# Even mixer: the S5 channels projected first, their passes beside the latent projections, scores two heads ahead

## The chip, the cores and the metric

One core of a Trainium2 chip runs the whole program. The metric is the device time of one execution in microseconds, the median of a few runs. Five engines work side by side and each takes its instructions in order: TensorE (PE in the rows) multiplies and transposes, VectorE (DVE), ScalarE (ACT), GpSimd (POOL) and SyncE (SP). SP, ACT and POOL also issue transfers, each in a queue of its own.

## The reference

The model has two layers: an even one (latent attention and S5 channels side by side) and an odd one (Hyena and RG-LRU), each between two SwiGLU half steps, over 256 latent and 256 context tokens. The change is in the even mixer:

```python
def even_mixer(h_ctx, h_lat, ...):
    cq_l, ckv_l, kr_l, s_l = jnp.split(h_lat @ w_in, cut, axis=-1)   # 384 | 256 | 32 | 512, the same for ctx
    k, v = mla_keys_values(ckv, kr, kv_norm, w_ukv, cos, sin)        # rmsnorm(ckv) @ w_ukv, rotary on kr
    q = mla_queries(cq, q_norm, w_uq, cos, sin)                      # rmsnorm(cq) @ w_uq, rotary on the last 32
    o_lat = latent_attention(...)                                    # 8 heads, softmax over ctx + lat
    s_ctx_out, ctx_finals = s5_stream(s_c, ..., None)                # 32 groups of 16 channels, 64 states,
    s_lat_out, _ = s5_stream(s_l, ..., ctx_finals)                   # both directions; then
    # y = gelu(C h + d * u);  y = y * sigmoid(y @ w_glu + b_glu)
    y_lat = jnp.concatenate([o_lat, s_lat_out], axis=-1) @ w_out
```

## The kernel before

Activations lie transposed, channels on partitions and the 512 tokens (256 of context, 256 latent) along the free axis. Products in f32 precision are three fp32r matmuls of high and low parts (`mm3`, L160 to L162); `split` (L166, L167) makes the parts, the high one on ACT, the low one on DVE.

The even mixer runs in these steps. `norm_proj` normalises the stream and beside that computes three of the ten 128-channel blocks of the input projection `ev_in`; the tuple `EVEN` says which. Blocks 7 and 8 are ckv, 4 to 6 are cq, 9 is kr, 0 to 3 are the S5 input u. Then come the remaining blocks; `low_norm` normalises ckv and cq (statistics by a matmul with a column, L255, the reciprocal root in small DVE steps, its rows by a matmul with the identity, L284, and the scaling with a split, L780). The four blocks of u are written to the DRAM tile `d_u` and read back in another layout (`ut`, L806).

S5 works in eight passes of four groups. `s5_states` loads two operands, mb and et, and does eight matmuls of 64 columns (L986, L988), a complex rotation, a scan (L1003) and a rotation back on DVE. `s5_out` loads gm and tz and does twelve matmuls (L1025 to L1027); tz is read from the padded rows of `d_v` in eight overlapping pieces (L1021). Its result goes to `d_y`. These loads stand on SP's queue, among the weight loads (`wload`, L144). The passes are laid beside other work: the states of pass i, then a product of queries or the scores of a head, then the output of pass i - 1.

A head is `scores` (matmuls L907, maximum on DVE, Exp on ACT L916, reciprocal on DVE L919, scaling on ACT L925 and DVE), `probs_t` (transposes L940, L946, copies on ACT L941, L947) and, for two heads at once, `values` (L959). The scores of a head are issued before the transposes of the head ahead. Behind the heads `s5_act` reads y back, adds the skip and applies Gelu (L1045), `s5_glu` does the gate (Sigmoid, L1063), and `out_proj` ends the mixer. Exp, Gelu and Sigmoid each need their table on ACT; a change of table is an instruction, ACT_TABLE_LOAD.

The tiles come from pools of a few buffers by tag ("x", "q", "p", "c"). A scheduler orders each engine's instructions from the order in which the code issues them and from priorities.

Of the kernel before, what the change touches and what calls it, by code (L numbers as in the profile page):

```python
# [18 lines left out]
P = 128  # L19
D = 1024  # L20
# [7 lines left out]
H = 8  # L28
# [37 lines left out]
class Builder:  # L66
# [581 lines left out]
    def s5_chunk(self, q):  # L648
# [93 lines left out]
    def s5_prepare(self):  # L742
        dt = lambda nm, shape: [self.dram.tile(shape, F32, tag=f"{nm}{q}", name=f"{nm}{q}") for q in range(NPASS)]
        self.d_mb = dt("d_mb", [P, 8, P])
        self.d_g = dt("d_g", [P, 8, P])
        self.d_v = dt("d_v", [P, 240])
        self.d_e = dt("d_e", [P, 2, 8, 64])
        yield from self.s5_small()
        for q in range(NPASS):
            yield from self.s5_chunk(q)  # L750


    def even_mixer(self):
# [19 lines left out]
        def low_norm(tiles, inv, g0):  # L773
            acc = self.slot("p", [P, T2])
            for i, x in enumerate(tiles):
                self.square_add(acc, x, i == 0)
            rb = self.rstd([acc], inv)
            o = []
            for i, x in enumerate(tiles):
                nc.vector.scalar_tensor_tensor(x, x, qn[:, g0 + i : g0 + i + 1], rb, op0=ALU.mult, op1=ALU.mult)  # L780
                y = self.slot("c", [P, 2, T2], F32R)
                self.split(y[:, 0, :], y[:, 1, :], x)
                o.append(y)
            return o

        ckv = low(pss[:2])
        cq = low(pss[2:] + [self.proj("ev_in", i, xs, 0, T2) for i in (5, 6)])
        st["kr"] = self.slot("kr", [P, T2])
        self.rope(st["kr"], self.proj("ev_in", 9, xs, 0, T2), ropet)

        d_u = self.dram.tile([512, L, NCH], F32, name="d_u")
        d_y = self.dram.tile([NG, L, 16, NCH], F32, name="d_y")
        ut = [self.slot("x", [P, 16, NCH]) for _ in range(2)]
        for i in range(4):
            u = self.slot("q", [P, L, NCH])
            nc.scalar.copy(u, self.proj("ev_in", i, xs, 0, T2).rearrange("p (c s) -> p s c", s=L))
            nc.scalar.dma_start(d_u[i * P : (i + 1) * P], u)
            if i == 0:
                st["ckv"] = low_norm(ckv, self.inv_kv, 3)
            elif i == 1:  # L800
                st["cq"] = low_norm(cq, self.inv_q, 0)
# [25 lines left out]
        def keys(p):  # L827
            k = self.slot("q", [P, 2, T2])
            ps = self.pm()
            self.mm3(ps, self.wparts(st["wk"], 2, o=p * 256), self.parts(st["ckv"], 0, T2))  # L830
            for h in range(2):
                nc.scalar.copy(k[0:64, h, :], ps[h * 64 : (h + 1) * 64])
                nc.gpsimd.dma_start(k[64:96, h, :], st["kr"][64:96])
            return k

        def queries(p):
# [5 lines left out]
                self.rope(q[:, h, :], ps, ropet)  # L842
            return q

        vt = values_in()
        st["wk"] = self.wload(t["wuk"], D)
        qs, ks = [], []
        passes = iter(range(NPASS + 1))
        state = [None]


        def s5_begin():
            i = next(passes, None)
            state.append(None if i is None or i == NPASS else self.s5_states(i, ut))
            return i

        def s5_end(i):
            if i:
                self.s5_out(i - 1, ut, d_y, state[i])

        for p in range(4):
            ks.append(keys(p))
            i = s5_begin() if p else None
            qs.append(queries(p))
            s5_end(i)
        os = []
        pend = None
        for h in range(H + 1):
            i = s5_begin()
            pr = self.scores(qs[h // 2][:, h % 2, :], ks[h // 2][:, h % 2, :]) if h < H else None  # L870
            s5_end(i)
            if h == H:
                fin = self.s5_act(d_u, d_y)
            if pend is not None:
                pts = self.probs_t(pend)
                if h % 2 == 1:
                    first = pts
                else:
                    os.append(self.values(h - 2, vt, (first, pts)))
            pend = pr  # L880
        os += self.s5_glu(*fin)
        self.out_proj("ev_out", 0, os, both, self.t["wgu"][1, 0, 0])

    def rope(self, o, ps, ropet):
# [86 lines left out]
    def s5_states(self, q, ut):  # L971

        nc = self.nc
        mb = self.slot("x", [P, 8, P])
        nc.sync.dma_start(mb, self.d_mb[q])
        et = self.slot("x", [P, 2, 512])
        nc.sync.dma_start(et, self.d_e[q].rearrange("p e g c -> p e (g c)"))
# [11 lines left out]
        ta, tb = self.slot("x", [P, 2, 512]), self.slot("x", [P, 2, 512])  # L989
# [11 lines left out]
        nc.gpsimd.memset(rz[:, :, 0:1], 0.0)  # L1001
# [6 lines left out]
        nc.gpsimd.memset(hv[:, :, 0:1], 0.0)  # L1008
        nc.vector.tensor_add(hv[:, :, 1:NCH], xv[:, :, 0 : NCH - 1], yv[:, :, 0 : NCH - 1])
        return hv  # L1010

    def s5_out(self, q, ut, d_y, hv):
        nc = self.nc
        u = ut[q // 4][:, (q % 4) * 4 : (q % 4) * 4 + 4, :]
        rev = lambda a: a.rearrange("p (t c) -> p t c", t=2)[:, :, ::-1]
        gm = self.slot("x", [P, 8, P])
        nc.sync.dma_start(gm, self.d_g[q])
        tz = self.slot("x", [P, 4, P])
        dv = self.d_v[q].rearrange("(g c) m -> c g m", g=4)[0:16]
# [12 lines left out]
    def s5_act(self, d_u, d_y):
        nc, t = self.nc, self.t
# [547 lines left out]
```

## Time and profile before

| | |
|---|---|
| median of 3 runs | 1765.29 us (1762.47 to 1765.68) |
| profiled execution | 1764.04 us, span 1762.0 us |
| TensorE busy | 1702.8 us, 97% of the span, mean granted clock 0.99 |
| VectorE busy | 1267.6 us, 72% |
| ScalarE busy | 693.7 us, 39% |
| GpSimd busy | 13.2 us, 1% |
| even mixer, first statistics matmul to that of the next ffn | 411 to 670 us of the span |

The span is the time from the first to the last instruction of the profiled execution. A busy TensorE is one on which a matmul is under way; at a granted clock of 1.00 it runs at 2.4 GHz, at 0.50 at 1.2 GHz.

### The profile page before, as it was taken

The page shows a single profiled execution, that of the slowest core. Times are in us where ns is not written, and L with a number is a line of the kernel's source. Part 1 is how long each engine was busy: PE and PEld are TensorE (multiplying, and loading weights), DVE is VectorE, ACT ScalarE, POOL GpSimd, SP SyncE. Part 2 cuts the span into 40 slices and gives each one's busy share as a digit, 9 for nine tenths or more (in the row PEclk, how much of TensorE's full clock was granted, in tenths as well). Part 3 has the DMA queues.
Part 4 walks back from the last instruction along what each step waited for, and adds up shares of the span by engine and source line. Part 5 has one row for each costly group of instructions (what it writes and reads, how often), then busy time and mean ns, then how long its engine had stood idle before and what let it go on. Part 6 is the DMA issues. An engine that isn't in the chain of part 4 may idle for free.

```text
span 1762.0 us, 24867 instructions
## 1 busy us (share of the span) xinstructions
PE 1702.8 (97%) x9380; PEld 1443.5 (82%) x9380; DVE 1267.6 (72%) x2545; ACT 693.7 (39%) x1101; POOL 13.2 (1%) x47
## 2 busy tenths in 40 slices
PE   5999999999989999999999999999999999699998
PEld 3788878889878788778888888888888888499998
DVE  7999999987488668776676686555543576976675
ACT  4433333443445654222222233222222357554443
POOL 0000000000000000000000000000000000000000
PEclk9999999999998999999999999999999999899999
DMA  9566767662465453564554443555533225155552
GB/s 330 172 221 213 228 212 229 215 189 95 126 188 166 132 188 107 171 216 147 164 190 157 159 141 124 181 185 155 169 120 96 96 96 187 67 171 189 183 183 90
DMA packets 107480, 292.65 MB, mean 166 GB/s; under 512 B 21152, under 2 KB 35360, under 8 KB 107104
## 3 DMA queue, kind: packets, MB, share of 16 engines
q1 hardware_dynamic: 101504, 286.86, 50.6%
q10 hardware_dynamic: 5216, 2.62, 0.8%
q0 software_dynamic: 640, 1.57, 0.3%
q8 instruction: 74, 1.21, 0.3%
q14 instruction: 46, 0.38, 0.1%
HBM read 272.20 MB, written 18.28 MB: 165 GB/s over the span
## 4 chain that ended last, share of the span: by engine, by line
PE 89%; DVE 6%; DMA 2%; issue 1%; SPq 1%; ACT 1%; DVEq 0%; ACTq 0%
PE mm L160 25%; PE mm L162 25%; PE mm L161 25%; PE mm L157 7%; DVE w L151 1%; DMA h<-in_modw_dram 1%; PE mm L1207 1%; SPq L1040 1%; DMA x<-d_g 1%; PE mm L907 1%; DVE x L322 0%; DVE nt L315 0%; PE mm L191 0%; PE ps L690 0%; PE ps L1118 0%
## 5 line engine op out<-in xcount | busy, mean ns | idle before, releaser
L150 ACT CAST w<-raw 128x1024 fp32r<-128x1024 f32 (+2 forms) x324 | 328.8, 1019 | 530.6 <-PE mm L162 262.2
L161 PE MATMUL mm<-x,w 128*128 128x512 f32 (+1 forms) x1424 | 519.8, 365 | 0.0
L162 PE MATMUL mm<-x,w 128*128 128x512 f32 (+1 forms) x1424 | 519.2, 365 | 0.0
L160 PE MATMUL mm<-x,w 128*128 128x512 f32 (+1 forms) x1424 | 514.6, 367 | 3.5 <-ACT x L320 2.2
L151 DVE TENSOR_TENSOR w<-raw,w 128x1024 fp32r<-128x1024 f32 (+2 forms) x324 | 383.8, 1186 | 150.5 <-ACT w L150 149.3
L160 PEld LDWEIGHTS mm<-x,w 128*128 128x128 f32 x1424 | 267.4, 189 | 49.5 <-ACT x L320 2.5
L161 PEld LDWEIGHTS mm<-x,w 128*128 128x128 f32 x1424 | 268.6, 189 | 43.8 <-issue 2.0
L162 PEld LDWEIGHTS mm<-x,w 128*128 128x128 f32 x1424 | 268.5, 189 | 43.9 <-issue 1.2
L227 DVE CUSTOM_DVE_ANT_0 junk<-m,sc 128x1024 f32<-128x1024 f32 x224 | 273.0, 1219 | 1.8 <-DMA m<-in_modw_dram 0.4
L160 PE MATMUL mm<-h,w 128*128 128x512 f32 x456 | 178.3, 394 | 0.0
L162 PE MATMUL mm<-h,w 128*128 128x512 f32 x456 | 176.9, 390 | 0.0
L161 PE MATMUL mm<-h,w 128*128 128x512 f32 x456 | 176.7, 390 | 0.0
L435 DVE SCALAR_TENSOR_TENSOR res<-mm,mraw,res 128x256 f32<-128x256 f32 x192 | 86.0, 479 | 96.5 <-PE mm L162 87.2
L471 DVE TENSOR_TENSOR h<-h,mm 128x512 f32<-128x512 f32 x66 | 45.3, 686 | 108.1 <-PE mm L162 95.8
L470 ACT ACTIVATE h<-mm 128x512 f32<-128x512 f32 x66 | 39.5, 598 | 196.0 <-PE mm L162 185.2
L160 PEld LDWEIGHTS mm<-h,w 128*128 128x128 f32 x456 | 85.6, 188 | 18.9 <-issue 1.1
L162 PEld LDWEIGHTS mm<-h,w 128*128 128x128 f32 x456 | 85.6, 188 | 18.5 <-issue 0.6
L161 PEld LDWEIGHTS mm<-h,w 128*128 128x128 f32 x456 | 85.6, 188 | 18.4 <-issue 1.0
L160 PE MATMUL mm<-hy,w 128*128 128x258 f32 x352 | 99.2, 284 | 0.7 <-DVE g L499 0.7
L162 PE MATMUL mm<-hy,w 128*128 128x258 f32 x352 | 99.6, 283 | 0.0
L161 PE MATMUL mm<-hy,w 128*128 128x258 f32 x352 | 99.6, 283 | 0.0
L157 PE MATMUL mm<-x,w 128*128 128x256 f32 x384 | 66.3, 290 | 6.7 <-DVE x L322 6.2
(371 smaller groups left out, 2002.1 us busy)
## 6 DMA issues: line engine op xcount, KB each, us to landing
raw<-in_wgu_dram SPq DMA_DIRECT2D x176, 512.0 KB, 3.9
m<-in_modw_dram SPq DMA_DIRECT2D x130, 512.0 KB, 4.3
raw<-in_wd_dram SPq DMA_DIRECT2D x64, 512.0 KB, 3.6
raw<-in_wd_dram SPq DMA_DIRECT2D x32, 384.0 KB, 3.3
raw<-in_od_in_dram SPq DMA_DIRECT2D x20, 512.0 KB, 3.5
h<-in_modw_dram SPq DMA_DIRECT2D x12, 512.0 KB, 10.0
raw<-in_ev_in_dram SPq DMA_DIRECT2D x10, 512.0 KB, 3.5
d_mb<-mbt SPq DMA_DIRECT2D x16, 256.0 KB, 3.4
```

Of the source, the lines that this page charges most:

```text
L150: nc.scalar.copy(hi[:, :n], raw[:, :n])
L151: nc.vector.tensor_sub(lo[:, :n], raw[:, :n], hi[:, :n])
L157: mm = lambda *a, **k: self.keep(self.nc.tensor.matmul(*a, **k))
L160: mm(ps, lhsT=wh, rhs=xh, start=first and i == 0, stop=False)
L161: mm(ps, lhsT=wh, rhs=xl, start=False, stop=False)
L162: r = mm(ps, lhsT=wl, rhs=xh, start=False, stop=last and i == n - 1)
L227: nc.vector.tensor_tensor_reduce(self.junk, w, self.sc[:, v, :], 1.0, 0.0, ALU.mult, ALU.add, raw[:, dt, v : v + 1])
L435: self.nc.vector.scalar_tensor_tensor(r, ps[:, c0:c1], gate[:, i, VEC[h] : VEC[h] + 1], r, op0=ALU.mult, op1=ALU.add)
L470: nc.scalar.activation(s[:, 0, lo:hi], pg[:, lo:hi], AF.Silu)
L471: nc.vector.tensor_mul(s[:, 1, lo:hi], s[:, 0, lo:hi], pu[:, lo:hi])
L907: nc.tensor.matmul(ps, lhsT=q[0:96, c : c + P], rhs=k[0:96, :nk], start=True, stop=True)
L1040: nc.sync.dma_start(uy[g * 16 : (g + 1) * 16, 1, :].rearrange("p (s n) -> p s n", s=L), d_y[i * 8 + g].rearrange("s c n -> c s n"))
```

## The change

The S5 input blocks 0 to 2 are the ones that `norm_proj` computes; block 3 follows, and u is written and read back at once. The projections of ckv, cq and kr come behind. The first passes of S5 stand beside those projections, the values and the keys, the last beside the scores of heads 2 to 5 (states up to head 4, the last output with head 5), where before they went on to the last head. `low_norm` is a generator in two pieces, the statistics and the scaling. The scores of head 0 are issued before the queries of the last two pairs, and the loop over heads starts at 1. `s5_act` is still issued when the scores of all heads are. The S5 operands are loaded on POOL's queue, those of passes 0 and 1 into buffers of tag "q"; tz is one load from a new DRAM tile `d_z`, which `s5_chunk` fills during the first ffn with four DRAM-to-DRAM transfers for each pass. The rotary part of the keys is copied by DVE instead of a transfer, two memsets of a pass move from POOL to DVE, and the write to `d_y` moves from POOL's queue to ACT's.

```diff
-EVEN, ODD = (7, 8, 4), (12, 13, 14)
+EVEN, ODD = (0, 1, 2), (12, 13, 14)
...
+        dv = self.d_v[q]
+        for g in range(4):
+            nc.gpsimd.dma_start(
+                self.d_z[q][:, g, :].rearrange("(r c) m -> r c m", r=L),
+                bass.AP(dv.tensor, dv.offset + g * 32 * 240, [[16, L], [240, 16], [1, P]]),
+            )
...
-            rb = self.rstd([acc], inv)
+            stats = self.rstd_stats([acc], inv)
+            yield
+            rb = self.rstd_rows(*stats)
...
-        ckv = low(pss[:2])
-        cq = low(pss[2:] + [self.proj("ev_in", i, xs, 0, T2) for i in (5, 6)])
...
-            nc.scalar.copy(u, self.proj("ev_in", i, xs, 0, T2).rearrange("p (c s) -> p s c", s=L))
+            nc.scalar.copy(u, (pss[i] if i < 3 else project(i)).rearrange("p (c s) -> p s c", s=L))
...
-                nc.gpsimd.dma_start(k[64:96, h, :], st["kr"][64:96])
+                nc.vector.tensor_copy(k[64:96, h, :], st["kr"][64:96])
...
-        for p in range(4):
-            ks.append(keys(p))
-            i = s5_begin() if p else None
-            qs.append(queries(p))
-            s5_end(i)
...
+        ckv = low([project(7), project(8)])
+        norm = low_norm(ckv, self.inv_kv, 3)
+        cq = [with_pass(lambda: project(4))]
+        next(norm)
+        cq.append(project(5))
+        st["ckv"] = next(norm)
+        cq = low(cq + [with_pass(lambda: project(6))])
...
+        norm = low_norm(cq, self.inv_q, 0)
+        st["wk"] = self.wload(t["wuk"], D)
+        next(norm)
+        vt = with_pass(values_in)
+        ks.append(keys(0))
+        st["cq"] = next(norm)
+        with_pass(lambda: ks.append(keys(1)))
+        qs.append(queries(0))
+        qs.append(queries(1))
+        score = lambda h: self.scores(qs[h // 2][:, h % 2, :], ks[h // 2][:, h % 2, :])
+        pend = score(0)
+        with_pass(lambda: pair(2))
+        pair(3)
         os = []
-        for h in range(H + 1):
-            i = s5_begin()
-            pr = self.scores(qs[h // 2][:, h % 2, :], ks[h // 2][:, h % 2, :]) if h < H else None
-            s5_end(i)
-            if h == H:
+        for h in range(1, H + 1):
+            pr = None
+            if h < H:
+                pr = with_pass(lambda: score(h)) if 1 < h < 6 else score(h)
+            else:
                 fin = self.s5_act(d_u, d_y)
...
-        gm = self.slot("x", [P, 8, P])
-        nc.sync.dma_start(gm, self.d_g[q])
-        tz = self.slot("x", [P, 4, P])
-        dv = self.d_v[q].rearrange("(g c) m -> c g m", g=4)[0:16]
-        for r in range(L):
-            nc.sync.dma_start(tz[r * 16 : (r + 1) * 16], dv[:, :, r * 16 : r * 16 + P])
+        gm = self.slot(tag, [P, 8, P])
+        nc.gpsimd.dma_start(gm, self.d_g[q])
+        tz = self.slot(tag, [P, 4, P])
+        nc.gpsimd.dma_start(tz, self.d_z[q])
...
-        nc.gpsimd.dma_start(d_y[q * 4 : (q + 1) * 4].rearrange("g s c n -> (s c) g n"), ys)
+        nc.scalar.dma_start(d_y[q * 4 : (q + 1) * 4].rearrange("g s c n -> (s c) g n"), ys)
```

On SP before, the loads of the second S5 output stood behind three loads of out-projection weights:

```order
L144 DMA raw_5802<-in_ev_out_dram 128x1024
L144 DMA raw_5840<-in_ev_out_dram 128x1024
L144 DMA raw_5878<-in_ev_out_dram 128x1024
L1017 DMA x_4845<-d_g_139 128x1024
L1021 DMA x_4847<-d_v_147 16x4x128 x8
```

The operands of that pass's output (d_g, d_z) and of the states of passes 2 and 3 (d_mb, d_e) now stand on POOL's queue:

```order
L994 DMA x_4595<-d_mb_132 128x1024
L996 DMA x_4597<-d_e_164 128x1024
L1037 DMA q_4484<-d_g_138 128x1024
L1039 DMA q_4486<-d_z_154 128x512
L1037 DMA q_4662<-d_g_139 128x1024
L1039 DMA q_4664<-d_z_155 128x512
L994 DMA x_4710<-d_mb_133 128x1024
L996 DMA x_4712<-d_e_165 128x1024
```

No weight load stands among them, and the output of a pass takes two loads where it took nine.

On DVE, the norm of the queries (L780, in the change L790: three scalings of cq by its row of reciprocal roots, then three splits L167) stood in a row before:

```order
L780 SCALAR_TENSOR_TENSOR p_4183<-p_4183,qkvn,ps_4356 128x512 x2
L780 SCALAR_TENSOR_TENSOR p_4186<-p_4186,qkvn,ps_4356 128x512
L167 TENSOR_TENSOR c_4397<-p_4183,c_4397 128x512
L167 TENSOR_TENSOR c_4401<-p_4183,c_4401 128x512
L167 TENSOR_TENSOR c_4405<-p_4186,c_4405 128x512
```

The changed kernel has S5 operations of passes 2 and 3 between them (x and hh are S5 tiles):

```order
L1022 SCALAR_TENSOR_TENSOR x_4609<-x_4609,x_4608 128x512
L790 SCALAR_TENSOR_TENSOR p_4504<-p_4504,qkvn,ps_4559 128x512 x2
L790 SCALAR_TENSOR_TENSOR p_4507<-p_4507,qkvn,ps_4559 128x512
L1023 TENSOR_TENSOR x_4608<-x_4609,x_4597 128x512
L1013 TENSOR_TENSOR x_4608<-x_4609,x_4597 64x512
L1014 TENSOR_TENSOR x_4608<-x_4609,x_4597 64x512
L167 TENSOR_TENSOR c_4699<-p_4504,c_4699 128x512
```

The first low part of cq, c_4699, has moved from right behind the scalings to behind three more instructions. On TensorE the first rows behind the row matmuls of this norm are now eight of an S5 pass and the query products:

```order
L284 MATMUL ps_4559<-ident,rs_y_4566 128x128 x4
L1005 MATMUL ps_4714<-x_4162,x_4710 128x64 x4
L1007 MATMUL ps_4714<-x_4162,x_4710 128x64 x4
L160 MATMUL mm_4776<-c_4699,w_4772 128x512
L160 MATMUL mm_4792<-c_4699,w_4772 128x512
L160 MATMUL mm_4814<-c_4699,w_4810 128x512
L160 MATMUL mm_4830<-c_4699,w_4810 128x512
L161 MATMUL mm_4776<-c_4699,w_4772 128x512
```

Before, the corresponding L284 row had thirteen 512-wide matmuls of values and keys and seven of S5 between it and the first query product.

On ACT, the end of the heads before: the last Exps and their scaling (L916, L925), the copies of the last transposes (L941, L947), and behind them one table load for the first Gelu (L1045):

```order
L916 ACTIVATE p_5536,sm_st_5537<-mm_5538,sm_st_5537 128x512
L916 ACTIVATE p_5536,sm_st_5537<-mm_5540,sm_st_5537 128x512
L925 ACTIVATE p_5536<-p_5536,sm_st_5537 128x512 x2
L1029 COPY ys_5350<-ps_5337 128x256
L947 COPY c_5557<-mm_5564 128x4x128
L941 COPY c_5632<-mm_5633 128x512
L1029 COPY ys_5439<-ps_5426 128x256
L947 COPY c_5639<-mm_5640 128x4x128
L1045 ACT_TABLE_LOAD
L1045 ACTIVATE x_5572<-x_5572 128x512
```

In the changed kernel a Gelu (L1063) stands three times among the Exps of heads 5 to 7 (L934, scaling L943, copies L959, L965); this is the second time, and the first stands two Exps before:

```order
L934 ACTIVATE p_5392,sm_st_5393<-mm_5396,sm_st_5393 128x512
L1047 COPY ys_5423<-ps_5410 128x256
L959 COPY c_5426<-mm_5427 128x512
L965 COPY c_5433<-mm_5434 128x4x128
L943 ACTIVATE p_5392<-p_5392,sm_st_5393 128x512 x2
L1048 DMA d_y<-ys_5423 128x4x64
L965 COPY c_5433<-mm_5440 128x4x128
L1063 ACT_TABLE_LOAD
L1063 ACTIVATE x_5571<-x_5571 128x512
L934 ACT_TABLE_LOAD
L934 ACTIVATE p_5446,sm_st_5447<-mm_5448,sm_st_5447 128x256 x2
L166 CAST x_5583<-x_5571 128x512
```

ACT has 23 table loads in all where it had 17.

## Rows read from the trace of the kernel before

**Rows 1.** Busy time by window (us, instructions), granted clock, DMA share, GB/s.

```profile
core 0: us, PE busy (x) PEld busy (x) DVE busy (x) ACT busy (x) POOL busy (x), PEclk, DMA share, GB/s
526.90:544.00 17.10, 13.75 (x58) 12.91 (x59) 12.62 (x26) 8.68 (x22) 1.01 (x3) 0.50 0.64 190
544.00:619.00 75.00, 72.72 (x480) 55.85 (x478) 54.13 (x108) 47.50 (x107) 5.42 (x14) 1.00 0.47 134
```

**Rows 2.** Timeline of TensorE, 513 to 548: start, us, line, out<-in, [idle <-releaser].

```profile
515.63 0.33 PE L1025 MATMUL ps<-x,x 128*128 128x64 f32 x2
...
518.26 1.06 PE L986 MATMUL ps<-x,x 128*128 128x64 f32 x8
...
520.05 2.80 PE L907 MATMUL mm<-q,q 96*128 96x256 f32 x8
530.25 0.66 PE L1025 MATMUL ps<-x,x 128*128 128x64 f32 x2 [7.40 <-DMA x<-d_v]
...
545.20 0.60 PE L940 MATMUL mm<-ident,p 128*128 128x128 f32 x4
...
546.51 0.33 PE L1025 MATMUL ps<-x,x 128*128 128x64 f32 x2
```

**Rows 3.** Timeline of SP's queue, 515 to 546.

```profile
514.75 8.33 SPq L144 DMA_DIRECT2D raw<-in_ev_out_dram  x3
523.17 0.38 SPq L1017 DMA_DIRECT2D x<-d_g  x1
523.66 4.75 SPq L1021 DMA_DIRECT2D x<-d_v  x8
```

**Rows 4.** Windows as in rows 1, two stretches of the odd mixer.

```profile
1503.20:1506.60 3.40, 2.92 (x4) 1.36 (x5) 3.40 (x6) 3.38 (x7) 0.00 (x0) 0.51 0.46 149
1516.80:1523.60 6.80, 3.42 (x8) 2.80 (x9) 6.80 (x12) 2.17 (x4) 0.00 (x0) 0.50 0.00 0
```

**Rows 5.** Timeline of DVE, 470 to 500.

```profile
486.15 2.06 DVE L780 SCALAR_TENSOR_TENSOR p<-p,qkvn,ps 128x512 f32<-128x512 f32 x3 [2.44 <-PE ps L284]
...
497.51 0.69 DVE L997 TENSOR_TENSOR x<-ps,x 128x512 f32<-128x512 f32 x1
```

**Rows 6.** Window as in rows 1, projection matmuls of 512 columns alone.

```profile
445.37:457.00 11.63, 11.63 (x53) 9.64 (x52) 4.37 (x4) 4.98 (x9) 0.00 (x0) 1.00 0.51 149
```

**Rows 7.** Timeline of ACT's own queue of transfers, 440 to 482.

```profile
469.35 0.33 ACTq L797 DMA_DIRECT2D d_u<-q  x1
471.38 3.50 ACTq L806 DMA_DIRECT2D x<-d_u  x7
```

**Rows 8.** Transfers, 411 to 670: queue, count, KB each, median us to landing.

```profile
x<-d_u ACTq DMA_DIRECT2D x16, 64.0 KB, 4.0
...
d_y<-ys POOLq DMA_DIRECT2D x8, 128.0 KB, 2.9
```

**Rows 9.** Timeline of ACT, 560 to 622.

```profile
566.53 0.58 ACT L947 COPY c<-mm 128x512 f32<-128x512 f32 x1
567.00 0.48 ACT L916 ACTIVATE p<-mm,sm_st 128x256 f32<-128x256 f32 x1
...
567.91 0.60 ACT L947 COPY c<-mm 128x512 f32<-128x512 f32 x1
568.47 0.69 ACT L916 ACTIVATE p<-mm,sm_st 128x512 f32<-128x512 f32 x1
...
569.14 0.68 ACT L916 ACTIVATE p<-mm,sm_st 128x512 f32<-128x512 f32 x1
...
572.51 1.33 ACT L925 ACTIVATE p<-p,sm_st 128x512 f32<-128x512 f32 x2 [2.60 <-DVE sm_st L919]
...
602.45 1.28 ACT L1045 ACT_TABLE_LOAD   x1
603.75 0.63 ACT L1045 ACTIVATE x<-x 128x512 f32<-128x512 f32 x1
```

**Rows 10.** Timeline of TensorE, 594 to 612: value products of two heads.

```profile
604.90 1.94 PE L959 MATMUL mm<-c,v 128*64 128x256 f32 x14 [1.22 <-ACT c L947]
```

**Rows 11.** Timeline of POOL, 440 to 620.

```profile
563.63 0.75 POOL L1030 DMA_DIRECT2D d_y<-ys  x1 [2.85 <-ACT ys L1029]
```

More of the change, by code (lines that the diff above doesn't have):

```diff
@@ L746, in s5_prepare @@
         self.d_v = dt("d_v", [P, 240])
+        self.d_z = dt("d_z", [P, 4, P])
         self.d_e = dt("d_e", [P, 2, 8, 64])
@@ L783, in low_norm @@
                 o.append(y)
-            return o
-        ckv = low(pss[:2])
-        cq = low(pss[2:] + [self.proj("ev_in", i, xs, 0, T2) for i in (5, 6)])
-        st["kr"] = self.slot("kr", [P, T2])
-        self.rope(st["kr"], self.proj("ev_in", 9, xs, 0, T2), ropet)
+            yield o
         d_u = self.dram.tile([512, L, NCH], F32, name="d_u")
@@ L793, in even_mixer @@
         ut = [self.slot("x", [P, 16, NCH]) for _ in range(2)]
+        project = lambda i: self.proj("ev_in", i, xs, 0, T2)
         for i in range(4):
             u = self.slot("q", [P, L, NCH])
-            nc.scalar.copy(u, self.proj("ev_in", i, xs, 0, T2).rearrange("p (c s) -> p s c", s=L))
+            nc.scalar.copy(u, (pss[i] if i < 3 else project(i)).rearrange("p (c s) -> p s c", s=L))
             nc.scalar.dma_start(d_u[i * P : (i + 1) * P], u)
[L798 to L801, printed above, removed]
             if i % 2:
@@ L843, in queries, with with_pass @@
             return q
-        vt = values_in()
-        st["wk"] = self.wload(t["wuk"], D)
         qs, ks = [], []
-        passes = iter(range(NPASS + 1))
         state = [None]
[L852 to L857, printed above, removed]
+        def with_pass(work):
+            i = len(state) - 1
+            state.append(self.s5_states(i, ut) if i < NPASS else None)
+            r = work()
@@ L858, in s5_end, with pair @@
             if i:
                 self.s5_out(i - 1, ut, d_y, state[i])
-        for p in range(4):
+            return r
+        def pair(p):
             ks.append(keys(p))
-            i = s5_begin() if p else None
             qs.append(queries(p))
-            s5_end(i)
-        os = []
-        pend = None
-        for h in range(H + 1):
-            i = s5_begin()
-            pr = self.scores(qs[h // 2][:, h % 2, :], ks[h // 2][:, h % 2, :]) if h < H else None
-            s5_end(i)
-            if h == H:
-                fin = self.s5_act(d_u, d_y)
[L874 to L879, printed above, removed]
+        ckv = low([project(7), project(8)])
@@ new lines, in even_mixer @@
+        norm = low_norm(ckv, self.inv_kv, 3)
[4 more added lines that the diff above has]
+        cq = low(cq + [with_pass(lambda: project(6))])
+        st["kr"] = self.slot("kr", [P, T2])
+        self.rope(st["kr"], project(9), ropet)
+        norm = low_norm(cq, self.inv_q, 0)
[4 more added lines that the diff above has]
+        st["cq"] = next(norm)
@@ new lines, in even_mixer @@
+        with_pass(lambda: ks.append(keys(1)))
[5 more added lines that the diff above has]
+        pair(3)
+        os = []
+        for h in range(1, H + 1):
[3 more added lines that the diff above has]
+            else:
+                fin = self.s5_act(d_u, d_y)
+            pts = self.probs_t(pend)
+            if h % 2 == 1:
+                first = pts
+            else:
+                os.append(self.values(h - 2, vt, (first, pts)))
@@ L880, in even_mixer @@
             pend = pr
-        os += self.s5_glu(*fin)
+        os += list(self.s5_glu(*fin))
         self.out_proj("ev_out", 0, os, both, self.t["wgu"][1, 0, 0])
@@ L973, in s5_states @@
         nc = self.nc
[L974 to L977, printed above, removed]
+        tag = "q" if q < 2 else "x"
+        mb = self.slot(tag, [P, 8, P])
+        nc.gpsimd.dma_start(mb, self.d_mb[q])
+        et = self.slot(tag, [P, 2, 512])
+        nc.gpsimd.dma_start(et, self.d_e[q].rearrange("p e g c -> p e (g c)"))
         er, ei = et[:, 0], et[:, 1]
@@ L988, in s5_states @@
                 nc.tensor.matmul(o.rearrange("p (t c) -> p t c", t=2), lhsT=mb[:, k, :], rhs=rev(u[:, g, :]), start=True, stop=True)
-        ta, tb = self.slot("x", [P, 2, 512]), self.slot("x", [P, 2, 512])
+        ta, tb = self.slot(tag, [P, 2, 512]), self.slot(tag, [P, 2, 512])
         hh = self.slot("hh", [P, 512])
@@ L1000, in s5_states @@
         rz = tb[:, 1].rearrange("p (g c) -> p g c", g=8)
-        nc.gpsimd.memset(rz[:, :, 0:1], 0.0)
+        nc.vector.memset(rz[:, :, 0:1], 0.0)
         nc.scalar.copy(rz[:, :, 1:NCH], self.s5["rho"][:, q * 8 : q * 8 + 8].unsqueeze(2).to_broadcast([P, 8, NCH - 1]))
@@ L1007, in s5_states @@
         xv, yv = (a.rearrange("p (g c) -> p g c", g=8) for a in (x, y))
-        nc.gpsimd.memset(hv[:, :, 0:1], 0.0)
+        nc.vector.memset(hv[:, :, 0:1], 0.0)
         nc.vector.tensor_add(hv[:, :, 1:NCH], xv[:, :, 0 : NCH - 1], yv[:, :, 0 : NCH - 1])
@@ L1013, in s5_out @@
         nc = self.nc
+        tag = "q" if q < 2 else "x"
         u = ut[q // 4][:, (q % 4) * 4 : (q % 4) * 4 + 4, :]
         rev = lambda a: a.rearrange("p (t c) -> p t c", t=2)[:, :, ::-1]
-        gm = self.slot("x", [P, 8, P])
-        nc.sync.dma_start(gm, self.d_g[q])
-        tz = self.slot("x", [P, 4, P])
-        dv = self.d_v[q].rearrange("(g c) m -> c g m", g=4)[0:16]
-        for r in range(L):
-            nc.sync.dma_start(tz[r * 16 : (r + 1) * 16], dv[:, :, r * 16 : r * 16 + P])
+        gm = self.slot(tag, [P, 8, P])
+        nc.gpsimd.dma_start(gm, self.d_g[q])
+        tz = self.slot(tag, [P, 4, P])
+        nc.gpsimd.dma_start(tz, self.d_z[q])
         py = self.ps()
@@ L1055, in s5_glu @@
         by = lambda a, o: a.rearrange(f"p ({o}) -> p s c", s=L)
-        os = []
         for i in range(4):
@@ L1066, in s5_glu @@
             self.split(o[:, 0, :], o[:, 1, :], z)
-            os.append(o)
-        return os
+            yield o
     def hyena_prepare(self):
```

## The prediction

> **What bounds the kernel now.** The table of the page says that TensorE is busy nearly the whole span, so only time in which TensorE idles, or runs at the lower clock, can be given back. I read its waits in the even mixer (411 to 670 us) first. One is large: the first matmul of an S5 output (L1025) came after 7.40 us of idle, and its releaser is the load of x from d_v [rows 2]. SP's own timeline says why that load was late. SP issues in order; three loads of out-projection weights held its queue from 514.75 for 8.33 us, and only then did d_g and the eight small d_v loads go out, the eight alone taking 4.75 us [rows 3]. The windows show the second half of the price: from 526.9 to 544 the granted clock was 0.50, 1.2 GHz, and behind that 1.00 again [rows 1]. TensorE had idled through the first part of it and then did small S5 matmuls and transposes.
>
> The price of this stall, from starts of rows. The work from 530.25 to 545.20 is twelve S5-output matmuls, one pass of S5 states, one head's transposes and one head's scores: 14.95 us. The same at 2.4 GHz: outputs 515.63 to 518.26, 2.63; states 518.26 to 520.05, 1.79; scores 2.80; transposes 545.20 to 546.51, 1.31; together 8.53 [rows 2]. So the clock cost 14.95 - 8.53 = 6.42 on top of 7.40. From 544 to 619, where the heads end and the S5 gate begins, TensorE was busy 72.72 of 75.00 us: 2.28 idle [rows 1].
>
> **What the change removes.** The Toeplitz operand is one load of the d_z copy, in place of eight, and the S5 operands stand on POOL's queue, where no weight load stands ahead of them. If they arrive in time, 7.40 and 6.42 go. The 2.28 lie in the stretch whose order on ACT is new; I count them as gone and price that stretch whole below. Gain: 7.40 + 6.42 + 2.28 = **16.1 us**.
>
> **What it moves at no cost.** TensorE's own work is the same, matmul for matmul. DVE and ACT gain small work (sixteen memsets and eight rotary copies on DVE), of which TensorE waits for nothing that the order shows. The thirty-two DRAM-to-DRAM copies for d_z run in the first ffn; nobody reads them for tens of us there, and if that cover failed, the first S5 output would wait as it did before. The latent norm of the keys is split: behind its row matmuls stand eight S5 and twelve projection matmuls, 1.79 + 2.6, and DVE needs two scalings, three S5 operations and one split, about 6 x 0.69 = 4.1. Covered.
>
> **What it adds, and where.**
> 1. *The norm of the queries.* Before, thirteen matmuls of values and keys stood behind the norm's row matmuls (L284). Now only the eight of an S5 pass do, 1.79 us, and then four query products that need the rounded high parts alone: 53 such matmuls take 11.63 us [rows 6], 0.22 each, so 0.9. DVE has three scalings, 2.06, then three S5 products of 0.69, and the low part that the fifth query product needs stands behind them: 2.06 + 2.07 + 0.69 = 4.8 [rows 5]. Wait: 4.8 - 2.7 = 2.1, and up to two more S5 operations of the pass in front of the row matmuls, 3.5. DVE's order has such operations ahead too, so I take 3.3.
> 2. *The end of the heads.* Three Gelus now stand between Exps of heads 5 to 7, and each costs a table load to Gelu and one back to Exp: six that were not there. A load took 1.28, and the Gelu began 0.02 after it ended; rows of ACT start about 0.1 before the one ahead ends [rows 9]. From the first of these loads to the first copy of the last head's transposed probabilities ACT has, start to start: six loads of 1.30, 7.8; three Gelus of 0.53, 1.6; sixteen copies and casts of 0.47, 7.5; three pairs of 512-wide Exps with accumulator reads at 0.67 each, 4.0; two 256-wide pairs of 0.91, 1.8; three scalings of 1.23, 3.7. Sum 26.4. In the same stretch TensorE has one S5 output, 2.63; four heads' transposes, 4 x 1.31 = 5.2; two heads' scores and a third of one, 6.5; nineteen value products of 0.27 (1.94 for seven), 5.1 [rows 2, 10]. Sum 19.5. Without the loads ACT would need 18.6 and fit under TensorE; with them ACT is the bound, and TensorE idles at least 26.4 - 19.5 = 6.9. ACT itself may wait for DVE's reciprocal, 2.60 once before [rows 9]; that gives 9.5 at most. ACT takes its queue in order and has transposes to wait for as well, so I take 9.0. It shows as idle ahead of transposes and values, in pieces of 3 to 5 us.
>    The Trainium skill, ScalarE: Activation LUTs, section What ACT_TABLE_LOAD costs, has about 1.28 us of load and 1.38 of drain, 2.66 for each switch of sets, and so speaks against this order; by that page six switches are 16 us, by the row 7.8. No drain stands behind the load in this trace [rows 9].
> 3. *The clock after those idles.* Nearest rows: in the odd mixer two short stretches at half clock, with 2.92 and 3.42 us of TensorE's work in them, cost half of that, 1.5 to 1.7 [rows 4]; the stall above cost 6.42. The work behind the new idles is the kind that stood behind the 7.40 (transposes, scores, an S5 output), so nearer to the upper: 4.5, with 1.5 and 6.4 as ends.
> 4. *The loads of u.* A pass cannot start before u has gone to d_u and come back in eight loads on ACT's queue. From the last early projection: two copies and a weight cast, an estimate of 2 from the 0.58 of a copy [rows 9]; the write, 2.0 from its issue to the first load; eight issues of 0.5, 4.0; landing 4.0; sum 12 [rows 7, 8]. TensorE has 72 projection matmuls in front, 72 x 0.22 = 15.8 [rows 6]. Covered by 3.8 us. Writes and landings that are 2 or 3 us slower each would leave 0 to 2 to pay; I take 0.5.
>
> Cost: 3.3 + 9.0 + 4.5 + 0.5 = **17.3**. Net 17.3 - 16.1 = +1.2. The profiled execution took 1764.04 (span 1762.0 and 2.04 around it), so 1765.2; it stood 1.25 under the median of its three runs, so the forecast for a median is 1766.5: **no change that the measurement can tell**. It tells about 0.2% of this kernel, 3.5 us: faster below 1761.8, slower above 1768.8. Ends: costs 2.1 + 6.9 + 1.5 + 0 = 10.5 give 1759.7; 3.5 + 9.5 + 6.4 + 2 = 21.4 give 1770.6.
>
> **Rivals.**
> A, *the gain is kept*: the table loads fall into time in which ACT would wait anyway, the tail keeps its 2.28, and the clock stays up. Net 3.3 + 0.5 - 13.8 = -10.0, 1755.3. For it: ACT is busy 47.50 of 75.00 us from 544 to 619 [rows 1], so it has free time on the average. Against: an in-order queue can use free time only where it lies, and in this stretch the sum is 26.4 against 19.5. It decides where TensorE has over 7 us of work that needs none of these ACT rows.
> B, *the half clock stays to the end of the heads*: the idles recur before TensorE gets dense work, as it stayed for 17.1 us after the 7.40. The 19.5 us of work then take 39, of which up to 9.0 fill the idle: +10.5 where I counted 4.5; 1772.5. For it: transposes and S5 matmuls alone stood in the stretch that stayed at 0.50. Against: value products and gate projections follow here. It decides if the granted clock is 0.5 for over 12 us.
> C, *the loads on POOL come late*: before, a 128 KB transfer on POOL's queue took 0.75 to issue and 2.9 to land [rows 8, 11]; each pass now needs three of 512 KB and one of 256 KB. If issue grows with size that is 3 x 3.0 + 1.5 = 10.5 us of queue, where passes beside heads come some 15 us apart (515.63, 530.25, 546.51) [rows 2]. It decides if a pass takes under 10.5; then an S5 wait of 3 to 7 us is back and the change has not done what it says: 1770 to 1774. Against: the order puts operands of the states ahead of those of the outputs, so most have a pass of lead. The Trainium skill, SBUF — State Buffer, section Who interferes with whom, says that transfers of the GpSimd queue starve for descriptors while DVE runs a two-port copy, and those of other queues don't; rows of before show no POOL issue beside a long DVE copy. Without that rule C has the same price.
> D, *the drain*, as that page has it: each switch costs 1.36 more than the row shows, 8.2 over six: 1774.7. Against it is the row itself.
>
> **Chances.** Forecast 0.60 (of it 0.49 within 0.2%, 0.04 below, 0.07 above, since its ends pass the bound on both sides); A 0.15; B 0.13; C 0.09; D 0.03. Faster 0.04 + 0.15 = 0.19; within 0.2% 0.49; slower 0.07 + 0.13 + 0.09 + 0.03 = 0.32. The range has to hold eight in ten: the forecast's ends and B, 1759.5 to 1773, with A, D and the worst of C outside.
>
> **What the profile of the changed kernel would show.** Right: no wait of an S5 output for its loads; no stretch at 0.50 around 530; six more table loads between Exp rows; TensorE idle for 7 to 9.5 us in all in the last heads, released by ACT's copies or scalings; 2 to 3.5 us ahead of the query products, released by DVE; a half-clock stretch of some us there. Wrong: the last heads without idle (A), a clock of 0.5 over the whole end (B), S5 matmuls that wait for transfers of POOL's queue (C), gaps on ACT behind its table loads (D), or a wait of the first S5 matmul for u.

## The result, and the profile after

The changed kernel took 1773.95 us (1773.52 to 1777.33), beside 1764.78 for the kernel before on the same chip: ratio 1.0058, 95% interval 1.0041 to 1.0076. It is slower by 9 us, outside the range and on the side of the rivals. The profiled execution's span is 1772.4 us, 10.4 more than before.

The mixer shows where. From the last wait for L322 ahead of it to the same wait of the next ffn, 430.65 to 677.77 before, it took 247.12 us; now, from 432.13 to 687.29, it takes 255.16. TensorE's timeline, first of the kernel before, then of the changed one:

```profile
430.65 0.50 PE L157 MATMUL mm<-x,w 128*128 128x256 f32 x2 [0.85 <-DVE x L322]
...
677.77 0.51 PE L157 MATMUL mm<-x,w 128*128 128x256 f32 x2 [0.85 <-DVE x L322]
```

```profile
432.13 0.50 PE L157 MATMUL mm<-x,w 128*128 128x256 f32 x2 [0.85 <-DVE x L322]
...
687.29 0.50 PE L157 MATMUL mm<-x,w 128*128 128x256 f32 x2 [0.85 <-DVE x L322]
```

That is +8.04. Of the other 2.4 us of span, 1.5 come before 432 us; in the profiled runs below, where no tile was added, this row lay at 430.4 to 433.6. The rest, 0.9, comes behind this mixer, in work that the change doesn't touch.

No S5 matmul waits for a transfer any more; the 7.40 of [rows 2] is gone. TensorE's timeline (the idle ahead of a row and its releaser in brackets) has new waits in three places: around the norm of the queries, at the first heads, and at the last ones.

```profile
502.81 1.22 PE L284 MATMUL ps<-ident,rs_y 128*128 128x128 f32 x8 [0.60 <-DVE rs_y L275]
506.07 1.20 PE L160 MATMUL mm<-c,w 128*128 128x512 f32 x4 [0.32 <-ACT c L166]
509.46 0.50 PE L161 MATMUL mm<-c,w 128*128 128x512 f32 x1 [2.20 <-DVE c L167]
...
544.28 0.63 PE L964 MATMUL mm<-ident,p 128*128 128x128 f32 x4 [1.50 <-DVE nt L909]
...
546.76 1.98 PE L925 MATMUL mm<-q,q 96*128 96x512 f32 x4 [0.76 <-ACT p L934]
...
551.21 0.66 PE L964 MATMUL mm<-ident,p 128*128 128x128 f32 x4 [2.03 <-ACT p L943]
...
597.22 2.97 PE L977 MATMUL mm<-c,v 128*64 128x256 f32 x10 [3.62 <-ACT p L934]
...
611.39 1.97 PE L964 MATMUL mm<-ident,p 128*128 128x128 f32 x8 [4.64 <-ACT p L943]
```

The windows (us, busy time of PE, PEld, DVE, ACT, POOL, then granted clock) answer to [rows 1]: TensorE ran at 0.50 for 6.8, 3.4 and 6.8 us behind these waits, and DVE was busy 39.29 of 41 us from 500 on and 10.63 of the next 11.

```profile
552.40:559.20 6.80, 6.80 (x32) 5.57 (x32) 4.51 (x11) 4.98 (x14) 2.12 (x4) 0.50 0.31 88
596.80:600.20 3.40, 2.98 (x11) 1.13 (x11) 1.54 (x5) 3.40 (x10) 0.00 (x0) 0.50 0.31 69
610.40:617.20 6.80, 5.81 (x17) 4.14 (x18) 1.43 (x3) 5.72 (x9) 0.00 (x0) 0.50 0.00 0
...
500.00:541.00 41.00, 37.89 (x216) 31.55 (x215) 39.29 (x84) 17.25 (x42) 6.17 (x12) 1.00 0.48 157
541.00:552.00 11.00, 6.71 (x43) 4.90 (x42) 10.63 (x24) 7.15 (x19) 0.00 (x0) 1.00 0.53 191
```

How DVE makes the heads late is read from ACT's timeline and DVE's. Head 0 comes first: ACT finished the 512-wide Exps of head 0 at 534.76. Their reciprocal (L937) is one DVE row of 0.17 us, and it came at 539.70, behind S5 rows and rotary rows that stood ahead of it; the scaling (L943) could start only then. That is the 2.63 in ACT's row. TensorE's three waits follow further on, each from a late DVE row. The 1.50 ahead of 544.28 ended with a rotary row (L909, at 543.70). The 0.76 ahead of 546.76 is a wait for head 1's Exps, which had themselves stood 2.92 us for the end of DVE's maximum (L932). The 2.03 ahead of 551.21 is a wait for head 1's scaling, whose reciprocal came at 550.25, behind S5 rows again.

```profile
534.56 0.20 ACT L934 ACTIVATION_READ_ACCUMULATOR p<-mm,sm_st 128x1 f32 x1
...
539.90 1.33 ACT L943 ACTIVATE p<-p,sm_st 128x512 f32<-128x512 f32 x2 [2.63 <-DVE sm_st L937]
...
545.68 0.47 ACT L934 ACTIVATE p<-mm,sm_st 128x256 f32<-128x256 f32 x1 [2.92 <-DVE sm_st L932]
...
550.44 1.33 ACT L943 ACTIVATE p<-p,sm_st 128x512 f32<-128x512 f32 x2 [0.92 <-DVE sm_st L937]
```

```profile
538.54 0.68 DVE L1014 TENSOR_TENSOR x<-x,x 64x512 f32<-64x512 f32 x1
539.25 0.42 DVE L910 TENSOR_TENSOR q<-q,nt 32x256 f32<-32x256 f32 x1
539.70 0.17 DVE L937 RECIPROCAL sm_st<-sm_st 128x2 f32<-128x2 f32 x1
...
543.70 0.43 DVE L909 TENSOR_TENSOR nt<-mm,rope 32x256 f32<-32x256 f32 x1
...
548.92 0.68 DVE L1014 TENSOR_TENSOR x<-ps,x 64x512 f32<-64x512 f32 x1
...
550.25 0.15 DVE L937 RECIPROCAL sm_st<-sm_st 128x2 f32<-128x2 f32 x1
```

At the end of the heads ACT's timeline shows what the prediction had priced, a Gelu between two table loads in front of the Exps of a head, with no gap behind a load:

```profile
592.91 1.28 ACT L1063 ACT_TABLE_LOAD   x1
594.21 0.63 ACT L1063 ACTIVATE x<-x 128x512 f32<-128x512 f32 x1
594.86 1.28 ACT L934 ACT_TABLE_LOAD   x1
596.15 0.47 ACT L934 ACTIVATE p<-mm,sm_st 128x256 f32<-128x256 f32 x1
```

### The profile page after: what moved, and what is told of

It is laid out like the page before. It is cut to its first block, busy times and chain, and to the rows that moved or that the text cites. A ratio compares the mean times of both kernels' runs of the same rounds, so it can differ in the third digit from the quotient of the medians.

```text
span 1772.4 us, 24789 instructions
## 1 busy us (share of the span) xinstructions
PE 1708.8 (96%) x9380; PEld 1445.0 (82%) x9380; DVE 1271.6 (72%) x2569; ACT 701.1 (40%) x1107; POOL 37.3 (2%) x79
## 4 chain that ended last, share of the span: by engine, by line
PE 89%; DVE 6%; ACT 2%; DMA 1%; issue 1%; SPq 0%; DVEq 0%; ACTq 0%
PE mm L160 25%; PE mm L161 25%; PE mm L162 25%; PE mm L157 7%; DVE w L151 1%; PE mm L977 1%; PE mm L1223 1%; PE mm L925 1%; DMA h<-in_modw_dram 1%; DMA raw<-in_wgu_dram 1%; DVE x L322 0%; DVE nt L315 0%; PE ps L690 0%; PE ps L1134 0%; PE mm L191 0%
## 5 line engine op out<-in xcount | busy, mean ns | idle before, releaser
L160 PE MATMUL mm<-x,w 128*128 128x512 f32 (+1 forms) x1424 | 517.3, 367 | 3.9 <-ACT x L320 3.0
L161 PE MATMUL mm<-x,w 128*128 128x512 f32 (+1 forms) x1424 | 520.6, 366 | 0.0
L162 PE MATMUL mm<-x,w 128*128 128x512 f32 (+1 forms) x1424 | 519.7, 365 | 0.0
L160 PEld LDWEIGHTS mm<-x,w 128*128 128x128 f32 x1424 | 268.2, 189 | 50.7 <-ACT x L320 3.3
L161 PEld LDWEIGHTS mm<-x,w 128*128 128x128 f32 x1424 | 269.1, 189 | 43.8 <-issue 2.0
L162 PEld LDWEIGHTS mm<-x,w 128*128 128x128 f32 x1424 | 268.9, 189 | 43.7 <-issue 1.2
L160 PE MATMUL mm<-h,w 128*128 128x512 f32 x456 | 178.3, 394 | 0.0
L162 PE MATMUL mm<-h,w 128*128 128x512 f32 x456 | 176.9, 390 | 0.0
L161 PE MATMUL mm<-h,w 128*128 128x512 f32 x456 | 176.7, 390 | 0.0
L160 PEld LDWEIGHTS mm<-h,w 128*128 128x128 f32 x456 | 85.6, 188 | 19.0 <-issue 1.1
L161 PEld LDWEIGHTS mm<-h,w 128*128 128x128 f32 x456 | 85.6, 188 | 18.4 <-issue 1.0
L162 PEld LDWEIGHTS mm<-h,w 128*128 128x128 f32 x456 | 85.6, 188 | 18.3 <-issue 0.6
L160 PE MATMUL mm<-hy,w 128*128 128x258 f32 x352 | 99.3, 284 | 0.3 <-DVE g L499 0.3
L162 PE MATMUL mm<-hy,w 128*128 128x258 f32 x352 | 99.6, 284 | 0.0
L161 PE MATMUL mm<-hy,w 128*128 128x258 f32 x352 | 99.6, 284 | 0.0
```

What stands on the lines that cost most here:

```text
L160: mm(ps, lhsT=wh, rhs=xh, start=first and i == 0, stop=False)
L161: mm(ps, lhsT=wh, rhs=xl, start=False, stop=False)
L162: r = mm(ps, lhsT=wl, rhs=xh, start=False, stop=last and i == n - 1)
```

## The experiments

All times are medians, each with the ratio to the kernel before on the same chip and the ratio's 95% interval. The median of the kernel before was 1764.78 to 1766.44 us over these series, so a difference between two experiments is good to about 2 us.

**The Gelus behind the heads.** The edit gives each Gelu a bias of zero that is made from the last head's last accumulator:

```diff
+            self.st_last = st
...
+        zero = self.small([P, 1], "gz", bufs=1)
+        nc.vector.tensor_scalar(zero, self.st_last[:, 2, 1:2], 0.0, None, op0=ALU.mult)
...
-            nc.scalar.activation(y, y, AF.Gelu_apprx_tanh)
+            nc.scalar.activation(y, y, AF.Gelu_apprx_tanh, bias=zero)
```

> The changed kernel with one edit: each Gelu adds a zero that is made from the accumulator of the last head's last Exp, so no Gelu can stand among the Exps. Theory: the six extra table loads make ACT the bound at the end of the heads; with them gone the 8.7 us of idle there shrink to 2 or 3 and the two half-clock stretches behind them (4.4 us) go, so 1764 to 1767. Rival, the Gelus were free where they stood: they now stand in a row ahead of the gate projections, whose wait takes the place, 1771 or more.

1788.85 us, 1.0122 (1.0105 to 1.0139): in neither of the two ranges. The idle at the end of the heads had fallen, but matmuls of the whole program, in the ffns too, had become slower. TensorE's timeline of this run, far from the edit, has starts 0.23 and 0.24 apart, where the changed kernel has 0.22 and 0.23:

```profile
720.30 0.39 PE L162 MATMUL mm<-x,w 128*128 128x512 f32 x1
720.54 0.40 PE L160 MATMUL mm<-x,w 128*128 128x512 f32 x1
720.77 0.39 PE L161 MATMUL mm<-x,w 128*128 128x512 f32 x1
```

The same edit with the zero kept in a column of the last head's small tile, so that no tile is added:

```diff
+        st = self.st_last
+        zero = st[:, 1, 1:2]
+        nc.vector.tensor_scalar(zero, st[:, 2, 1:2], 0.0, None, op0=ALU.mult)
```

> The run gelu_late again, but the zero for the Gelus is written into a small tile that is there already, in place of a new tile of 4 bytes a partition. In gelu_late every 512-wide matmul of the whole program came 0.233 us apart and not 0.227. If the new tile did that by shifting the tiles behind it, the pace is 0.227 again and the time 1763 to 1767, some 8 under the changed kernel, from the end of the heads. Rival, the bias operand of Gelu or its place costs: 1785 or more again.

1766.49 us, 1.0005 (0.9996 to 1.0014), 7.5 under the changed kernel. Its waits have 2.5 us for ACT's scaling, of which 2.04 belong to the first heads and 0.42 to the last, and 1.8 for a copy: 2.2 at the end of the heads, in place of 8.7. TensorE stood at half clock neither at 597 nor at 610; but from 509 to 512, behind the norm's wait, it did, where the changed kernel did not, and that took 1.5 us of the gain back:

```profile
PE mm L965 <- ACT p L944: 2.5, 2, 2.0
...
PE mm L978 <- ACT c L960: 1.8, 1, 1.8
PE mm L965 <- DVE nt L909: 1.5, 1, 1.5
```

The stall at the first heads is still there with the same lengths (1.50, 0.77, 2.04).

**The rotary copies off DVE.**

```diff
-                nc.vector.tensor_copy(k[64:96, h, :], st["kr"][64:96])
+                nc.gpsimd.dma_start(k[64:96, h, :], st["kr"][64:96])
```

> The changed kernel, with the rotary part of the keys copied by a POOL transfer as before, in place of eight DVE copies of 0.37 us. Theory: DVE is saturated from 482 to 557 us, and its backlog is the wait of 4.3 us at 541 to 552 with the half clock behind it (3.4): 3 us less on DVE take over half of that wait and the clock stretch away, 1767 to 1770. Rival, that wait is set by ACT or by the order of the scores: within 1 us of the changed kernel, 1773 to 1775.

1764.89 us, 0.9994 (0.9985 to 1.0003): 9 under the changed kernel, more than I expected. The scaling of head 0 stood at 531.33, right behind its Exps, and of the stall at the first heads 1.67 us and no half clock were left:

```profile
530.72 0.20 ACT L934 ACTIVATION_READ_ACCUMULATOR p<-mm,sm_st 128x1 f32 x1
531.33 1.35 ACT L943 ACTIVATE p<-p,sm_st 128x512 f32<-128x512 f32 x2
```

```profile
541.00:565.00 24.00, 22.33 (x151) 17.32 (x150) 20.91 (x47) 15.96 (x41) 2.23 (x4) 1.00 0.44 156
```

Not all of the gain lies there. Of the 8.6 us by which this mixer is shorter (255.16 to 246.59), 6.0 come from the first heads and 3.6 from the end of the heads, and 1.2 go back at the norm, to a half clock. At the end the edit changed ACT's order as well: the third Gelu's table load, at 600.47, now stands behind the last head's Exps, the run has 21 table loads where the changed kernel has 23, and the wait of 3.62 shrank to 0.3:

```profile
PE mm L977 <- ACT p L934: 0.3, 1, 0.3
```

To tell DVE from POOL's queue, the same copies on ACT (`nc.scalar.copy`):

> The changed kernel, with the rotary part of the keys copied by ACT. It takes the same 3 us off DVE as kr_by_dma, but leaves POOL's queue as the change has it. If DVE's backlog is what counts: 1763 to 1767, as kr_by_dma. If POOL's queue or its transfers made that run faster: 1772 to 1775.

1767.07 us, 1.0009 (0.9999 to 1.0018), at the edge of the range, with the wait at the first heads at 1.86, 3.4 us of half clock behind it, and 21 table loads too. So it is not POOL's queue that counts. DVE's busy time does not tell these runs apart: from 500 to 541 us it was 38.81 of 41 in kr_by_dma and 38.74 here, beside 39.29 in the changed kernel. An engine with work waiting is as busy with 3 us less of it; it is only further along. The row that ends DVE's maximum of head 1 (L932) came at 542.94 and 543.38, in the changed kernel at 545.49. And the opposite, each copy twice on DVE:

> The changed kernel, with each of the eight DVE copies of the rotary part done twice: 3 us more on DVE between 482 and 557 us. If DVE bounds that stretch, TensorE's idle there grows by some 3 us and the half clock with it: 1777 to 1782. If the waits there come from ACT or the order: 1773 to 1775.

1780.65 us, 1.0083 (1.0068 to 1.0098), as expected in size, but not by the way I expected. TensorE's idle in the mixer didn't grow. The wait for the norm changed into one of 1.86 for d_z, and from 500 to 520 us and again at the heads TensorE ran much longer at half clock; its mean granted clock from 500 to 520 was 0.66, beside 1.00 in the changed kernel.

At the first heads the idle was 2.84, less than the 4.29 of the changed kernel, although DVE had 3 us more to do; but while TensorE ran slowly DVE caught up, and stood idle for 2.55 us at 517. So this run is no evidence for or against the size of DVE's share.

**The first scores later.**

```diff
-        pend = score(0)
         with_pass(lambda: pair(2))
         pair(3)
+        pend = score(0)
```

> The changed kernel, with the first scores issued behind the queries of the last pair, not two pairs ahead. If the early scores cause the wait at 541 to 552 us, it goes with its half-clock stretch: 1766 to 1767. If DVE's total is the cause, the same work waits at another row: 1772 to 1775.

1773.4 us, 1.0035 (1.0022 to 1.0048): as DVE's total has it. The wait moved to an S5 output, whose states DVE now finished late:

```profile
PE ps L1044 <- DVE hh L1028: 4.0, 1, 4.0
```

**The loads alone.** In the kernel before, the S5 operands on POOL's queue and the Toeplitz operand from d_z, nothing else:

```diff
-        nc.sync.dma_start(mb, self.d_mb[q])
+        nc.gpsimd.dma_start(mb, self.d_mb[q])
...
-        for r in range(L):
-            nc.sync.dma_start(tz[r * 16 : (r + 1) * 16], dv[:, :, r * 16 : r * 16 + P])
+        nc.gpsimd.dma_start(tz, self.d_z[q])
```

> The kernel before, with one part of the change alone: the S5 operands on POOL's queue and the Toeplitz operand from d_z in one load; order, memsets and d_y writes as before. By the gain term of the prediction 7.40 + 6.42 go: 1751 to 1753. Rival: POOL's queue is in order too, and memsets and d_y writes that wait for TensorE and ACT stand ahead of the loads there, so an S5 wait of several us with half clock behind it returns: 1764 or more.

1773.49 us, 1.0039 (1.0024 to 1.0054): slower than before. POOL's timeline shows one reason. A memset that waits for TensorE and a d_y write that waits for ACT stand ahead of the next loads, d_z's at 523.26 among them, and TensorE then waits for d_z, 3.7 us in three waits:

```profile
521.24 0.11 POOL L1016 MEMSET hh<- 128x8 f32 x1 [13.27 <-PE ps L1033]
521.88 0.81 POOL L1036 DMA_DIRECT2D d_y<-ys  x1 [0.53 <-ACT ys L1035]
```

```profile
PE ps L1031 <- DMA x<-d_z: 3.7, 3, 2.4
```

Another 3.2 us are lost at the norm, in a wait for ACT that the next run has too.

With the memsets on DVE and the d_y writes on ACT's queue as well:

> The run loads_only with POOL's queue kept free: the two memsets of a pass on DVE and the d_y writes on ACT's queue, as in the change, the order of passes as before. If what stood ahead on POOL made the loads of loads_only late, no S5 matmul waits for a transfer any more, and the time falls under that run's 1773.5; the S5 wait of the kernel before is gone too, so 1751 to 1756 if nothing takes its place. Rival: with the passes still beside the queries and every head, DVE is late next there and the idle comes back at the transposes, 1762 to 1767.

1763.79 us, 0.9993 (0.9983 to 1.0002). No S5 matmul waits for a transfer, and still nothing is gained. Other waits took the place:

```profile
PE mm L954 <- ACT p L933: 3.3, 2, 2.2
PE mm L948 <- DVE p L931: 3.2, 1, 3.2
PE mm L160 <- ACT c L166: 2.9, 1, 2.9
```

At the heads, from 535 to 541 us, TensorE waited 3.16 for DVE's scaling and 1.09 for ACT's, whose Exps had stood for DVE's maximum; with the half clock from 538 to 545 that is 7.1 us. At 604 it waited 2.22 for ACT's scaling of a head, behind a Gelu between two table loads; this run has 19 of them, the kernel before 17. At the norm it waited 2.88, with 1.7 of half clock: ACT had stood 8.32 us ahead of that split, for loads of u.

```profile
495.96 0.62 ACT L166 CAST c<-p 128x512 fp32r<-128x512 f32 x1 [8.32 <-DMA x<-d_u]
```

Removing the wait of [rows 2] is worth nothing in this order, and about half of what took its place is DVE's. The windows of the kernel before had shown DVE's part, in rows that I had read and not used: all through the 7.40 us in which TensorE stood still, DVE was busy, 3.91 of 4.05 and 3.36 of 3.40.

```profile
522.85:526.90 4.05, 0.00 (x0) 0.00 (x0) 3.91 (x9) 1.01 (x5) 0.00 (x0) 1.00 0.75 268
526.90:530.30 3.40, 0.05 (x1) 0.08 (x1) 3.36 (x7) 1.34 (x5) 0.00 (x0) 0.50 0.55 113
```

**The loads of the changed kernel on SP's queue.** The four loads of a pass, d_z among them, with `nc.sync` in place of `nc.gpsimd`.

> The changed kernel with the S5 operands (d_z too, in one load) on SP's queue. If the queue is what removed the 7.40 us wait, an S5 wait for transfers of some us and its half clock return on top of the others: 1777 to 1785. If the new place of the passes (or the one load) did it, no S5 wait: 1770 to 1775.

1775.83 us (1769.38 to 1779.47), 1.0049 (1.0025 to 1.0072), between the two ranges. S5 matmuls wait for transfers again, 3.3 us in two waits, and SP's timeline has two weight loads in front that hold the queue for 9.54:

```profile
PE ps L1005 <- DMA x<-d_mb: 1.9, 1, 1.9
PE ps L1043 <- DMA x<-d_z: 1.4, 1, 1.4
```

```profile
488.24 9.54 SPq L144 DMA_DIRECT2D raw<-in_s_glu_dram  x2
```

The queue matters for the wait; the runs of this kernel scatter too widely to price it.

**Both edits.** Gelus last, copies by POOL's transfers:

> The changed kernel with the Gelus behind the last Exp (without a new tile) and the rotary part of the keys copied by POOL's transfers. Theory: the two costs are separate, DVE's backlog before the heads and the table loads at their end, so their gains add: 1773.9 less 9 less 7 to 8, 1756 to 1759, which beats both kernels. Rival, a wait or a half-clock stretch moves on to the next idle and only the larger of the gains is had: 1763 to 1766.

1760.63 us (1759.17 to 1762.94), 0.9974 (0.9962 to 0.9985): it beats both kernels, before by 0.26%. It fell short of the sum of the two gains (7.5 and 9.1) by 3. The gains overlap at the end of the heads: the 3.6 that kr_by_dma had gained there come from waits that the Gelus' move takes away too. What is left is 2.2 at the norm, 1.7 at the first heads and 2.2 at the end; the first and the last have 3.4 us of half clock behind them.

```profile
PE mm L161 <- DVE c L167: 2.2, 1, 2.2
PE mm L965 <- ACT p L944: 2.1, 2, 1.7
PE mm L978 <- ACT c L960: 1.8, 1, 1.8
```

**An added tile.** The changed kernel with one more small tile, set to zero once, of 4 bytes a partition and then of 64:

```diff
+        pad = self.small([P, 1], "gz", bufs=1)
+        nc.vector.memset(pad, 0.0)
```

> The changed kernel with nothing but one more tile of 4 bytes a partition in the pool of small tiles, set to zero once. If the shift of the tiles behind it slows the matmuls, as the run gelu_late suggests: pace 0.233 us and 1794 to 1800. If not: the changed kernel's 1774.

1797.75 us, 1.0185 (1.017 to 1.02). The tile alone does it. The group row of ffn matmuls has a mean of 395 ns, beside 389 for the changed kernel:

```profile
L161 PE MATMUL mm<-x,w 128*128 128x512 f32 x287 | 113.5, 395 | 0.0
```

> The run pad4 with the added tile at 64 bytes a partition, not 4. If an odd start address of the tiles behind it is what slows the matmuls: the changed kernel's time, 1772 to 1776. If any added tile does it: 1795 or more.

1780.95 us, 1.0083 (1.0068 to 1.0098): in neither of the two ranges. It is 17 us faster than with 4 bytes and still 7 slower than without, and one of its three kinds of matmul has the old mean (390 for L160, 392 for L161, 394 for L162). What about the added tile makes the difference was not settled.

## Why the prediction was wrong

Its steps, against the profile after:

- *The norm of the queries*: 3.3 forecast, 0.60 + 0.32 + 2.20 = 3.12 measured. The 0.60 stands ahead of the norm's row matmuls, where the sum had nothing; behind them it is 2.52.
- *The end of the heads*: 9.0 forecast. The waits there are 3.62 and 4.64 and one of 0.43 for a copy: 8.7. gelu_last shows that the Gelus with their table loads cause all but 2.2 of them. The Trainium skill's drain of each load (ScalarE: Activation LUTs, What ACT_TABLE_LOAD costs) is not in this trace: the Gelu at 594.21 starts 0.02 us after its load ends, the next load 0.02 after the Gelu ends, and the Exp at 596.15 0.01 after that load.
- *The clock behind those idles*: 4.5 forecast. At 0.50 TensorE was busy 2.98 and 5.81 us, half of which is 4.4.
- *The loads of u*: 0.5 forecast, no wait.
- *What it moves at no cost*: **the step that failed**. I priced DVE's added work at nothing, with the words that TensorE waits for nothing of it, from the order alone, and named only memsets and copies. The S5 passes that now stand beside the keys, queries and first scores bring DVE work too, and I did not add up its time there. From 482 to 500 us DVE was busy for 16.68 of 18 us, where it was 9.92 before, and for 39.29 of the next 41. The stall that followed at the first heads is 1.50 + 0.76 + 2.03 = 4.29 us of idle and half of 6.80 at the lower clock, 3.4: 7.7 us that the sum didn't have. Each of its three waits ended with a late DVE row, directly or by way of ACT.

Windows of DVE's time as above, first of the kernel before, then of the changed one:

```profile
482.00:500.00 18.00, 18.00 (x93) 15.26 (x92) 9.92 (x16) 10.75 (x21) 0.91 (x2) 1.00 0.79 197
```

```profile
482.00:500.00 18.00, 18.00 (x113) 16.03 (x113) 16.68 (x44) 8.95 (x17) 1.23 (x3) 1.00 0.60 229
```

With it the sum closes: 3.1 + 8.7 + 4.4 + 7.7 = 23.9, less the 16.1, is +7.8 beside a measured +8.04 for the mixer. So close a sum is in part luck: counted alike in both traces, TensorE's idle and its loss at half clock rose by 6.6 us in the mixer, and 1.4 of the 8.04 has no place in it. The gain term stood in the sense that the wait and its clock went. That this is gain only as far as nothing else is late behind it is the same error seen from the other side: in loads_free_queue DVE took half of it back, and ACT the rest.

The rivals: A and D are out. C's premise is wrong, because POOL's loads of 512 KB took 0.53 us to issue and not 3. B's time was near, but not its mechanism: the clock came back between the stalls.

What stays open: taking the copies off DVE also changed the order of DVE's rows, so that the reciprocal of head 0 came right behind its Exps, and ACT's order at the end of the heads. Whether the 3 us or the order is worth more of the 6.0 us at the first heads wasn't told apart; kr_twice was to do it and did not. That late DVE rows cause the stall rests on its three waits, on two runs that relieve DVE in different ways, and on score_late, where the wait moved to another DVE row and the time stayed.

## What to carry to other kernels

Before a stall is counted as gain, look at what the other engines do during it: an engine that is busy all through it may be the next bound, and work that is moved onto that engine can cost more than its own time, because an idle of TensorE can bring a stretch of half clock behind it. Add up every engine's work for the stretch, not only for the one that is seen to wait, and look at what stands ahead of the row that the others need: busy time alone didn't tell the stalled run from the relieved ones. The scheduler here put Gelus between Exps at the price of two table loads each; tie functions of another table behind the last use of the first. And read a small edit's gain stage by stage: taking eight copies off DVE also moved a Gelu on ACT, and over a third of the gain came from there.

## What the runs showed of the hardware

A tile of 4 bytes a partition, added to the pool of small tiles and used once, slowed the 512-wide matmuls from 389 to 395 ns in the mean, and the program by 24 us; one of 64 bytes cost 7 us. gelu_late, which adds the same 4 bytes, has 395 too. All other experiments leave the small tiles as they were, and their matmuls of this group stand at 389 or 390 ns as in both kernels. On POOL's queue the issue of a load took 0.53 us for 512 KB and 0.54 for 256 KB, less than the 0.75 of the 128 KB d_y write in [rows 11].
